# A hybrid decoder step on one core: sample y gathered in head pairs, fewer TensorE passes, and the sample states updated a token at a time on ScalarE and VectorE

## The chip, the cores and the metric

The kernel runs on one core of a Trainium2 chip. The time is device microseconds from launch to end, the median of several executions; lower is better. The core has TensorE (matrix products; PE in the profile, and PEld for its weight loads), VectorE (DVE), ScalarE (ACT), GpSimd (POOL) and SyncE (SP). In this kernel SP issues nearly all loads, POOL most stores, and each engine runs its instructions in the order in which they were emitted.

## The reference

One layer of a decoder step, for 256 prompt tokens and 8 sample sequences of 4 tokens each, 288 tokens in all. D_MODEL is 2048.

```python
h = rmsnorm(x)
u|v, z, xBC, dt, ga, gb = split(h @ w_in)
ya = u * (W_s @ layernorm(v) + b)                 # branch A, spatial gating
xs, B, C = split(silu(causal_conv(xBC)))          # branch B, Mamba-2: 64 heads, 8 groups
dt = softplus(dt + dt_bias); da = dt * -exp(a_log)
y = chunked_scan(xs, dt, da, B, C, h0) + d_skip * xs
yb = group_rmsnorm(y * silu(z))
x = x + (sigmoid(ga) * (ya @ w_out_a) + sigmoid(gb) * (yb @ w_out_b)) @ w_o
x = x + (silu(h2 @ w_gate) * (h2 @ w_up)) @ w_down   # h2 = rmsnorm(x)
y_out = rmsnorm(x)
```

The scan also gives the states after the last token. For a sample sequence that is, for each head, `state = state * exp(sum of da) + sum over its 4 tokens of (decayed dt*x) outer B`, with a state of 64 x 128 per head: 16 MB read and 16 MB written over the 8 sequences and 64 heads. This is the update that the change moves off TensorE.

## The kernel before, in words

All activations lie with channels in partitions and the 288 tokens in the free dimension. Every large product streams a weight matrix once, in units of 256 output columns. SP loads raw fp32 weights, 4 k (512 KB) at a time, into four buffers. ScalarE rounds each such piece to `wh` (line 183) and VectorE takes the rest `wl = raw - wh` (line 152); TensorE then makes three products of 288 columns for each 128x128 weight tile: `wh` with the high and the low part of the activations, and `wl` with the high part (line 187). So a piece is 24 products named pm, in one of two PSUM tiles ("m"). Three buffers hold `wh` and `wl`, and the split of a piece is emitted two pieces ahead, so a cast waits until the products of the piece three before it are done. The activations have names with h and l at the end: hh and hl for the normalised input, ybh and ybl for yb, xgh and xgl for the input of the FFN, fh and fl for its hidden layer.

The order of all engines is fixed when the program is built, by the class Plan. `units` walks through the units in an order written out by hand: v, dt, b, u, c, ga, the projection of branch A, then x and z, the first half of B (eight units, groups 0 to 3 of yb, one group for each piece), more x and z, gb, the second half of B, w_o, and the FFN. Between the k of a unit it calls `side`, which lets the generators of all other work run on: g_ssd, g_head, g_gate and so on, with priorities; the state update, g_upd, has the last but for nothing, 3, and starts at the mark "late", behind the z units. A generator goes on when the planner's own clocks say that what it waits for is ready, with a margin MG, and when VectorE and ScalarE are not planned more than SL = 2300 ns behind TensorE. Where TensorE is to use something that isn't emitted yet, `need` lets every generator run without that limit until it is. `res` and `rel` count the buffers: 25 large tiles q, 7 tiles t, 4 PSUM tiles x and 2 of m.

g_ssd prepares a group of 8 heads: cb = C'B, masked into cbm, the transposes btok, xt, xts, and the products for the prompt's last states (fin). g_head makes y of two heads (one of four pairs): a masked decay matrix m of 128 x 768, then on TensorE the sample's part from the old states (yoff times a selection), the sample's own part (a 32 x 64 slice of xts times a 32 x 32 block of ms), and the prompt's part (xt times m, 256 and 128 columns, for two halves of 64 rows). g_gate multiplies with silu(z), takes the group's mean square through a product with ones (rms) and a Newton iteration on VectorE and ScalarE, and writes ybh and ybl. g_upd forms, for each of 32 head pairs, the update of 8 states as two TensorE products of 512 columns (names up, from bk and sk), and VectorE adds them to the decayed states su, 8 instructions of 128x128; POOL stores 512 KB. At the end, fin_steps runs the prompt's last states while the final norm is taken, and SP stores y.

Of the kernel before, what the change touches and what calls it, by code (L numbers as in the profile page):

```python
# [6 lines left out]
F32 = mybir.dt.float32  # L7
# [50 lines left out]
class Plan:  # L58
# [216 lines left out]
    def rms(self, parts, scale, eps, out):  # L275
# [27 lines left out]
    def units(self, units, x_parts, first_loads):  # L303
# [35 lines left out]
        def split_to(i):  # L339
            while nxt[1] <= min(i, len(pieces) - 1):  # L340
# [3 lines left out]
                hi = self.wp.tile([128, NK, 256], F32R, tag="wh", name="wh")[:, 0:k1 - k0, 0:m]  # L344
                lo = self.wp.tile([128, NK, 256], F32R, tag="wl", name="wl")[:, 0:k1 - k0, 0:m]
# [3 lines left out]
                wt[nxt[1]] = (hi, lo)  # L349
# [6 lines left out]
        for i, (u, k0, k1, r, o) in enumerate(pieces):  # L356
# [28 lines left out]
def trunk(ctx, tc, io):  # L385
# [238 lines left out]
    def g_dt(ps):  # L624
# [200 lines left out]
    def g_ssd(g):  # L825
# [66 lines left out]
        yield ms  # L892
        K.mul(ms, ms, cbm[:, 384:416].unsqueeze(1).to_broadcast([128, 2, S]))
# [9 lines left out]
        for hf in range(2):  # L903
# [4 lines left out]
            left = [2]  # L908
            for j2 in range(2):
                K.spawn(1, g_head(g, hf, j2, csb, cbm, ms, xts, xt, X, left))  # L910

    def g_head(g, hf, j2, csb, cbm, ms, xts, xt, X, left):
        j = 2 * hf + j2
        m = yield from K.q([2, 384], f"m{g}{j}")
        yield csb
        for c in range(2):
            K.add(m[:, :, 256 * c:256 * c + 128], csb[:, 2 * j2:2 * j2 + 2, 128 * c:128 * c + 128], neg)
        yield m
        for i in range(2):
            h = 8 * g + 2 * j + i  # L920
            K.act(m[:, i, 0:128], m[:, i, 0:128], AF.Exp, bias=ncs[:, 0, h:h + 1])
            K.act(m[:, i, 128:256], csb[:, 2 * j2 + i, 128:256], AF.Exp, bias=dec[:, h:h + 1])
            K.act(m[:, i, 256:384], m[:, i, 256:384], AF.Exp, bias=ncs[:, 1, h:h + 1])
            yield None
        left[0] -= 1
        if not left[0]:
            K.drop()
# [524 lines left out]
```

## Time and profile before

| what | value |
| --- | --- |
| median of 3 runs | 2328.21 us (2327.59 to 2328.46) |
| profiled execution, its time | 2328.14 us |
| its span, first to last instruction | 2326.4 us |
| TensorE busy | 2317.5 us |
| VectorE busy | 1423.4 us |
| ScalarE busy | 996.9 us |
| GpSimd busy | 89.6 us |
| mean DMA rate | 196 GB/s |

The busy times come from one profiled execution. TensorE's is the time with at least one product under way; products overlap, so one of 288 columns shows as some 300 ns while the next one starts 133 ns later. The difference between time and span lies before the first and behind the last instruction.

### The profile page before, as it was taken

The page shows a single profiled execution, that of the slowest core. Times are in us where ns is not written, and L with a number is a line of the kernel's source. Part 1 is how long each engine was busy: PE and PEld are TensorE (multiplying, and loading weights), DVE is VectorE, ACT ScalarE, POOL GpSimd, SP SyncE. Part 2 cuts the span into 40 slices and gives each one's busy share as a digit, 9 for nine tenths or more (in the row PEclk, how much of TensorE's full clock was granted, in tenths as well). Part 3 has the DMA queues.
Part 4 walks back from the last instruction along what each step waited for, and adds up shares of the span by engine and source line. Part 5 has one row for each costly group of instructions (what it writes and reads, how often), then busy time and mean ns, then how long its engine had stood idle before and what let it go on. Part 6 is the DMA issues. An engine that isn't in the chain of part 4 may idle for free.

```text
span 2326.4 us, 42350 instructions
## 1 busy us (share of the span) xinstructions
PE 2317.5 (100%) x17523; PEld 2280.3 (98%) x17523; DVE 1423.4 (61%) x2174; ACT 996.9 (43%) x1413; POOL 89.6 (4%) x187
## 2 busy tenths in 40 slices
PE   9999999999999999999999999999999999999998
PEld 8999989999999999999999999999999999999998
DVE  7687553446878775477765777766554444544544
ACT  6443433335655554455433334433333333333332
POOL 0000000001100010010000000000000000000000
PEclk9999999999999999999999999999999999999999
DMA  8464685566665565564577877776555555555654
GB/s 284 139 207 147 204 296 169 179 187 186 194 226 170 155 196 182 179 191 137 172 236 250 277 269 256 234 240 228 181 167 159 167 170 167 166 164 165 231 168 135
DMA packets 150530, 455.26 MB, mean 196 GB/s; under 512 B 18736, under 2 KB 40496, under 8 KB 150336
## 3 DMA queue, kind: packets, MB, share of 16 engines
q1 hardware_dynamic: 139952, 423.35, 58.0%
q0 software_dynamic: 9376, 27.62, 3.2%
q8 instruction: 137, 2.24, 0.4%
q10 hardware_dynamic: 1008, 1.58, 0.2%
q14 instruction: 57, 0.47, 0.1%
HBM read 420.94 MB, written 31.54 MB: 194 GB/s over the span
## 4 chain that ended last, share of the span: by engine, by line
PE 99%; DMA 0%; ACT 0%; DVE 0%; SPq 0%; issue 0%; ACTq 0%
PE pm L187 93%; PE y L187 2%; PE yoff L187 1%; PE up L187 1%; PE fin L187 1%; PE mix L187 0%; PE xt L193 0%; PE cb L187 0%; DMA x<-x 0%; PE rms L187 0%; PE va L193 0%; PE btok L193 0%; ACT wh L183 0%; PE cst L187 0%; SPq L197 0%; PE vb L193 0%
## 5 line engine op out<-in xcount | busy, mean ns | idle before, releaser
L152 DVE TENSOR_TENSOR wl<-raw,wh 128x1024 fp32r<-128x1024 f32 (+2 forms) x704 | 837.9, 1190 | 860.8 <-ACT wh L183 851.5
L183 ACT CAST wh<-raw 128x1024 fp32r<-128x1024 f32 (+2 forms) x704 | 718.6, 1021 | 1111.3 <-PE pm L187 812.5
L187 PE MATMUL pm<-hh,wh 128*128 128x288 f32 x2128 | 635.5, 299 | 0.0
L187 PE MATMUL pm<-hh,wl 128*128 128x288 f32 x2128 | 628.1, 295 | 0.0
L187 PE MATMUL pm<-hl,wh 128*128 128x288 f32 x2128 | 627.7, 295 | 0.0
L187 PE MATMUL pm<-xgh,wl 128*128 128x288 f32 x1408 | 415.7, 295 | 0.0
L187 PE MATMUL pm<-xgl,wh 128*128 128x288 f32 x1408 | 415.6, 295 | 0.0
L187 PE MATMUL pm<-xgh,wh 128*128 128x288 f32 x1408 | 414.7, 295 | 0.0
L187 PEld LDWEIGHTS pm<-hh,wh 128*128 128x128 f32 x2128 | 399.8, 188 | 10.0 <-issue 8.4
L187 PEld LDWEIGHTS pm<-hl,wh 128*128 128x128 f32 x2128 | 399.6, 188 | 0.7
L187 PEld LDWEIGHTS pm<-hh,wl 128*128 128x128 f32 x2128 | 399.6, 188 | 0.2 <-DVE wl L152 0.2
L187 PEld LDWEIGHTS pm<-xgl,wh 128*128 128x128 f32 x1408 | 264.5, 188 | 0.6
L187 PEld LDWEIGHTS pm<-xgh,wh 128*128 128x128 f32 x1408 | 264.3, 188 | 0.6
L187 PEld LDWEIGHTS pm<-xgh,wl 128*128 128x128 f32 x1408 | 264.4, 188 | 0.0
L187 PE MATMUL pm<-fl,wh 128*128 128x288 f32 x704 | 207.8, 295 | 0.0
L187 PE MATMUL pm<-fh,wl 128*128 128x288 f32 x704 | 207.8, 295 | 0.0
L187 PE MATMUL pm<-fh,wh 128*128 128x288 f32 x704 | 207.2, 294 | 0.0
L187 PE MATMUL pm<-ybh,wh 128*128 128x288 f32 x512 | 152.1, 297 | 0.0
L187 PE MATMUL pm<-ybh,wl 128*128 128x288 f32 x512 | 151.1, 295 | 0.0
L187 PE MATMUL pm<-ybl,wh 128*128 128x288 f32 x512 | 151.0, 295 | 0.0
L187 PEld LDWEIGHTS pm<-fl,wh 128*128 128x128 f32 x704 | 132.3, 188 | 0.0
L187 PEld LDWEIGHTS pm<-fh,wl 128*128 128x128 f32 x704 | 132.2, 188 | 0.0
(249 smaller groups left out, 2802.2 us busy)
## 6 DMA issues: line engine op xcount, KB each, us to landing
raw<-w_in SPq DMA_DIRECT2D x284, 512.0 KB, 3.9
raw<-w_gu SPq DMA_DIRECT2D x176, 512.0 KB, 3.8
raw<-w_d SPq DMA_DIRECT2D x75, 512.0 KB, 3.6
raw<-w_b SPq DMA_DIRECT2D x64, 512.0 KB, 4.6
st<-st_n SPq DMA_DIRECT2D x32, 512.0 KB, 7.7
raw<-w_a SPq DMA_DIRECT2D x32, 512.0 KB, 3.7
su<-st_p SPq DMA_DIRECT2D x32, 512.0 KB, 5.6
new_ssm_s<-su POOLq DMA_DIRECT2D x32, 512.0 KB, 4.3
```

The costliest lines, as they stand in the source:

```text
L152: self.nc.vector.tensor_tensor(out, a, b, op=op)
L183: self.nc.scalar.copy(out, a)
L187: self.nc.tensor.matmul(out, lhsT, rhs, start=start, stop=stop)
```

## The change

Five things change.

- The sample's y is made for two head pairs at once (g_heads). The 32 x 32 blocks become full-height products: cbz holds the blocks of cb in their own rows and zeros elsewhere, mz is ms times cbz, and yoff, xts and m are all multiplied in column halves of 64 with all 128 rows. It takes two PSUM tiles x and two tiles q at a time.
- The dt unit loads 64 columns of weights in place of 128 and packs their two parts side by side, so one product with the high and one with the low part of h gives both; ScalarE and VectorE add the halves.
- A mean square of one part is rounded and split (rmp) and multiplied with a rounded matrix of ones: two products at the rounded rate in place of one in fp32.
- The state update leaves TensorE. The states lie in 64 tiles, one for a group and a sequence, 128 x 4 x 128. For each, SP loads the state, the four rows of B broadcast over all partitions (bx) and 16 columns of the weighted x, which TensorE now transposes once a group (xwt). ScalarE scales the four parts by the decay, VectorE adds the four tokens, 16 instructions `su <- bx * x + su`, and POOL stores 256 KB. The tiles come from the pool t; one tile is loaded ahead.
- The planner gets a clock for the DMA queues, and a higher cost for a VectorE instruction with a scalar read from memory.

```diff
-        self.clk = dict(pe=0.0, dve=0.0, act=0.0, pool=0.0)
+        self.clk = dict(pe=0.0, dve=0.0, act=0.0, pool=0.0, dma=0.0)
...
     def stt(self, out, a, s, b, op0, op1):
         self.nc.vector.scalar_tensor_tensor(out=out, in0=a, scalar=s, in1=b, op0=op0, op1=op1)
-        self._at("dve", (free(out) + 66) / 0.96 + 61 * (not isinstance(s, float)), [out], [a, b])
+        self._at("dve", (free(out) + 66) / 0.96 + 140 * (not isinstance(s, float)), [out], [a, b])
...
         (eng or self.nc.sync).dma_start(out=out, in_=a)
-        self.rdy[out.tensor.name] = self.clk["pe"] + 4000
+        self._moved(out)
+        self.rdy[out.tensor.name] = self.clk["dma"] + 4000
     def store(self, out, a, eng=None):
         (eng or self.nc.gpsimd).dma_start(out=out, in_=a)
+        self._moved(a)
+    def _moved(self, a):
+        self.clk["dma"] = max(self.clk["dma"], self.clk["pe"]) + a.shape[0] * free(a) * 4 / 370
...
-        ps = self.ps("rms")
-        for i, part in enumerate(parts):
-            self.mm(ps[:, 0:T], self.one, part, i == 0, i == len(parts) - 1)
+        if len(parts) == 1:
+            w = self.tmp([128, 2, T], "rmp", F32R)
+            self.hilo(w[:, 0], w[:, 1], parts[0])
+            yield w
+            ps = self.ps("rms")
+            for i in range(2):
+                self.mm(ps[:, 0:T], self.oner, w[:, i], i == 0, i == 1, f32=False)
+        else:
+            ps = self.ps("rms")
+            for i, part in enumerate(parts):
+                self.mm(ps[:, 0:T], self.one, part, i == 0, i == len(parts) - 1)
...
-                hi = self.wp.tile([128, NK, 256], F32R, tag="wh", name="wh")[:, 0:k1 - k0, 0:m]
-                lo = self.wp.tile([128, NK, 256], F32R, tag="wl", name="wl")[:, 0:k1 - k0, 0:m]
+                wh = self.wp.tile([128, NK, 256], F32R, tag="wh", name="wh")[:, 0:k1 - k0]
+                hi = wh[:, :, 0:m]
+                if m == 64:
+                    lo = wh[:, :, m:2 * m]
+                else:
+                    lo = self.wp.tile([128, NK, 256], F32R, tag="wl", name="wl")[:, 0:k1 - k0, 0:m]
...
                 xh, xl = self.acts[key]
+                if m == 64:
+                    self.mm(ps[:, 0, 0:T], lo[:, k - k0], xh, k == 0, False, f32=False)
+                    self.mm(ps[:, 0, 0:T], lo[:, k - k0], xl, False, k == nk - 1, f32=False)
...
-        K.act(x, ps[0:64, 0, 0:T], AF.Identity, bias=vec[0:64, V_DT:V_DT + 1])
+        K.act(x, ps[64:128, 0, 0:T], AF.Identity, bias=vec[64:128, V_DT:V_DT + 1])
+        yield x
+        K.add(x, x, ps[0:64, 0, 0:T])
...
-        cbm = K.tmp([128, 416 + 2 * S], "cbm")
-        ms = cbm[:, 416:416 + 2 * S].rearrange("p (i t) -> p i t", i=2)
-        K.mul(cbm[:, 0:416], p1[:, 0:416], masks)
+        cbm = K.tmp([128, 512 + 2 * S], "cbm")
+        cbz = cbm[:, 384:512].rearrange("p (j t) -> p j t", j=4)
+        ms = cbm[:, 512:512 + 2 * S].rearrange("p (i t) -> p i t", i=2)
+        K.mul(cbm[:, 0:384], p1[:, 0:384], masks)
+        K.mul(cbz, p1[:, 384:416].unsqueeze(1).to_broadcast([128, 4, S]), own)
...
-        xw = K.tmp([128, 128], "xw")
+        xws = K.tmp([128, 2, 128], "xw")
+        xw, xwt = xws[:, 0], xws[:, 1]
         K.mul(pair(xw), pair(xts), wide(wds[:, H2]))
-        K.store(io["scr_xs"][g], xw)
+        yield xw
+        p1 = K.ps("xwt")
+        K.tr(p1[:, 0:128], xw)
+        yield p1
+        K.copy(xwt.rearrange("p (b j l) -> p j b l", b=NB, j=4), p1[:, 0:128].rearrange("p (j b l) -> p j b l", j=4, b=NB))
+        K.store(io["scr_xs"][g], xwt)
...
-            left = [2]
-            for j2 in range(2):
-                K.spawn(1, g_head(g, hf, j2, csb, cbm, ms, xts, xt, X, left))
-    def g_head(g, hf, j2, csb, cbm, ms, xts, xt, X, left):
...
+            K.spawn(1, g_heads(g, hf, csb, cbm, cbz, ms, xts, xt, X))
+    def g_heads(g, hf, csb, cbm, cbz, ms, xts, xt, X):
+        ms_, mz = [], []
+        for j2 in range(2):
+            t = yield from K.q([768 + 2 * S], f"m{g}{2 * hf + j2}")
+            ms_.append(t[:, 0:768].rearrange("p (i t) -> p i t", i=2))
+            mz.append(t[:, 768:768 + 2 * S].rearrange("p (i t) -> p i t", i=2))
+            if not j2:
+                yield csb
+            for c in range(2):
+                K.add(ms_[j2][:, :, 256 * c:256 * c + 128], csb[:, 2 * j2:2 * j2 + 2, 128 * c:128 * c + 128], neg)
+        for j2, m in enumerate(ms_):
+            yield m
+            for i in range(2):
+                h = 8 * g + 2 * (2 * hf + j2) + i
+                K.act(m[:, i, 0:128], m[:, i, 0:128], AF.Exp, bias=ncs[:, 0, h:h + 1])
+                K.act(m[:, i, 128:256], csb[:, 2 * j2 + i, 128:256], AF.Exp, bias=dec[:, h:h + 1])
+                K.act(m[:, i, 256:384], m[:, i, 256:384], AF.Exp, bias=ncs[:, 1, h:h + 1])
+                yield None
         K.drop()
+        for j2, m in enumerate(ms_):
+            yield m
+            K.mul(m, m, cbm[:, 0:384].unsqueeze(1).to_broadcast([128, 2, 384]))
+            K.mul(mz[j2], ms, cbz[:, 2 * hf + j2].unsqueeze(1).to_broadcast([128, 2, S]))
+        yield ms_ + [yoff]
+        yield from K.res("x", 2)
+        pys = [K.ps("y") for _ in range(2)]
+        halves = [(i, slice(64 * i, 64 * i + 64)) for i in range(2)]
+        for j2, py in enumerate(pys):
+            j = 2 * hf + j2
+            for i, o in halves:
+                K.mm(py[o, P:T], yoff[:, g % NY, 128 * j + 64 * i:128 * j + 64 * i + 64], sel, True, False)
+            for i, o in halves:
+                K.mm(py[o, P:T], xts[:, o], mz[j2][:, i], False, True)
+        for j2, py in enumerate(pys):
+            j = 2 * hf + j2
+            for c in range(2):
+                for i, o in halves:
+                    hc = slice(128 * j + 64 * i, 128 * j + 64 * i + 64)
+                    K.mm(py[o, 128 * c:P], xt[:, c, hc], ms_[j2][:, i, 256 * c:256 + 128 * c], c == 0, c == 1)
+        K.drop(2)
+        heads_done[g] = heads_done.get(g, 0) + 2
         if heads_done[g] == 4:
             K.drop()
             K.rel("t")
             if g % 4 == 3:
                 K.drop()
+        for j2, py in enumerate(pys):
+            j = 2 * hf + j2
+            yield py
+            K.stt(X[:, j], X[:, j], vec[:, V_DS + 4 * g + j:V_DS + 4 * g + j + 1], py[:, 0:T], ALU.mult, ALU.add)
+            K.rel("x")
+            evac_done[g] = evac_done.get(g, 0) + 1
+            if evac_done[g] == 4:
+                K.have.add(f"ssd{g}")
...
-    def g_upd(g):
...
+    def upd_load(n):
+        g, b = divmod(n, NB)
+        yield f"fin{g}"
         yield from K.res("t", 2)
+        st, w = K.tmp([128, 4, 128], "su"), K.tmp([128, 528], "bx")
+        K.load(st, io["st_p"][n])
+        K.load(w[:, 0:512].rearrange("p (l n) -> p l n", l=L), io["scr_bs"][g, L * b:L * b + L].partition_broadcast(128))
+        K.load(w[:, 512:528], io["scr_xs"][g, :, 16 * b:16 * b + 16])
+        return st, w
+    def g_upd():
+        yield "late"
+        nxt = yield from upd_load(0)
+        for n in range(64):
+            g, b = divmod(n, NB)
+            st, w = nxt
+            if n < 63:
+                nxt = yield from upd_load(n + 1)
+            yield [st, w]
+            for j in range(4):
+                K.act(st[:, j], st[:, j], AF.Copy, scale=etot[:, 4 * g + j, b:b + 1])
             yield st
+            for l in range(L):
+                for j in range(4):
+                    K.stt(st[:, j], w[:, 128 * l:128 * l + 128], w[:, 512 + 4 * j + l:513 + 4 * j + l], st[:, j],
+                          ALU.mult, ALU.add)
+                yield None
             yield st
+            K.store(io["new_ssm_s"][n], st)
+            K.rel("t", 2)
+        K.have.add("upd")
...
-        K.spawn(3, g_upd(g))
+    K.spawn(3, g_upd())
...
-    dev["w_dt"] = ca(wt[:, :, 14336:14464].transpose(1, 0, 2))
+    dev["w_dt"] = ca(wt[:, :, 14336:14400].transpose(1, 0, 2))
...
-    dev["st_p"] = ca(f["state_ssm"][0].reshape(8, 32, 128, 128).transpose(1, 2, 0, 3))
+    dev["st_p"] = ca(f["state_ssm"][0].reshape(8, 8, 4, 128, 128).transpose(1, 0, 3, 2, 4).reshape(64, 128, 4, 128))
```

The order of TensorE inside the first unit of B (B0), before, where the products of group 2 end and those of group 3 begin (the number behind ybh and ybl is that of the tile):

```order
L187 MATMUL pm<-ybh_8494,wh 128x288
L187 MATMUL pm<-ybl_8495,wh 128x288
L187 MATMUL pm<-ybh_8494,wl 128x288
L187 MATMUL pm<-ybh_8835,wh 128x288
L187 MATMUL pm<-ybl_8836,wh 128x288
L187 MATMUL pm<-ybh_8835,wl 128x288
```

And after the change, at the same place of B0:

```order
L187 MATMUL pm<-ybh_8921,wl 128x288
L193 MATMUL btok<-cst,bf 128x128 x2
L193 MATMUL btok<-cst,bf 32x128
L193 MATMUL xt<-cst,xs_8720 128x128 x8
L193 MATMUL xts<-cst,sm 128x128
L187 MATMUL rms<-rmp,oner 128x288 x2
L193 MATMUL xwt<-cst,xw 128x128
L187 MATMUL pm<-ybh_9460,wh 128x288
L187 MATMUL pm<-ybl_9461,wh 128x288
L187 MATMUL pm<-ybh_9460,wl 128x288
```

In the new order the transposes of g_ssd of a later group, the sum rms of group 3 itself and the transpose xwt stand directly ahead of its products, since all that g_gate does for group 3 is emitted there.

VectorE, before, at the place where ybl of group 3 (ybl_8836) is written, ahead of the first B unit; wl<-raw,wh is the low part of a weight piece:

```order
L170 SCALAR_TENSOR_TENSOR xs_7302<-xs_7302,vec,rbg 128x288 x4
L152 TENSOR_TENSOR wl<-raw,wh 128x1024
L170 SCALAR_TENSOR_TENSOR acc<-cb,cwh,acc 128x312 x2
L152 TENSOR_TENSOR ybl_8836<-xs_7302,ybh_8835 128x576
L170 SCALAR_TENSOR_TENSOR acc<-cb,cwh,acc 128x312
L152 TENSOR_TENSOR wl<-raw,wh 128x1024
L170 SCALAR_TENSOR_TENSOR acc<-cb,cwh,acc 128x312 x3
L152 TENSOR_TENSOR wl<-raw,wh 128x1024
L152 TENSOR_TENSOR ybl_8836<-xs_7302,ybh_8835 128x576
L727 MEMSET cb 128x2x3
```

After, the rows at whose end ybl of group 3 (ybl_9461) is written, behind the start of unit B0; rbg and nt are the Newton iteration, m the decay matrices of the next group:

```order
L170 SCALAR_TENSOR_TENSOR rbg<-nt,rbg 128x288
L152 TENSOR_TENSOR m_9432<-csb_9340,cst 128x2x128 x2
L152 TENSOR_TENSOR m_9435<-csb_9340,cst 128x2x128 x2
L152 TENSOR_TENSOR nt<-nt 128x288
L170 SCALAR_TENSOR_TENSOR nt<-nt 128x288
L170 SCALAR_TENSOR_TENSOR rbg<-nt,rbg 128x288
L170 SCALAR_TENSOR_TENSOR xs_7203<-xs_7203,vec,rbg 128x288 x4
L152 TENSOR_TENSOR m_9432<-m_9432,cbm 128x768
L152 TENSOR_TENSOR m_9432<-cbm 128x64
L152 TENSOR_TENSOR ybl_9461<-xs_7203,ybh_9460 128x576 x2
L152 TENSOR_TENSOR m_9435<-m_9435,cbm 128x768
L152 TENSOR_TENSOR m_9435<-cbm 128x64
```

Before, the four multiplications with rbg and the two ybl rows stood between weight splits of units ahead of B0. Now no weight split stands among these rows, which follow each other from the Newton iteration to ybl.

VectorE at the first units of the FFN, before; ff<-pm,rb reads a finished unit out of PSUM:

```order
L152 TENSOR_TENSOR nt<-nt 128x288
L170 SCALAR_TENSOR_TENSOR nt<-nt 128x288
L170 SCALAR_TENSOR_TENSOR rb<-nt,rb 128x288
L170 SCALAR_TENSOR_TENSOR su_16211<-su_16211,etot,up_16272 128x128 x4
L170 SCALAR_TENSOR_TENSOR su_16211<-su_16211,etot,up_16273 128x128 x4
L152 TENSOR_TENSOR wl<-raw,wh 128x1024
L152 TENSOR_TENSOR ff<-pm,rb 128x288 x2
L152 TENSOR_TENSOR wl<-raw,wh 128x1024 x2
L152 TENSOR_TENSOR ff<-ff 128x288
L152 TENSOR_TENSOR ff<-pm,rb 128x288 x2
```

After:

```order
L152 TENSOR_TENSOR nt<-nt 128x288
L170 SCALAR_TENSOR_TENSOR nt<-nt 128x288
L170 SCALAR_TENSOR_TENSOR rb<-nt,rb 128x288
L152 TENSOR_TENSOR wl<-raw,wh 128x1024
L170 SCALAR_TENSOR_TENSOR su<-bx,su 128x128 x16
L152 TENSOR_TENSOR ff<-pm,rb 128x288 x4
L152 TENSOR_TENSOR wl<-raw,wh 128x1024 x3
L152 TENSOR_TENSOR ff<-ff 128x288 x2
```

The 16 rows of a whole update tile now stand between a weight split and the rows that read the units out.

VectorE at the end of the program, before; x<-x,r is the last multiplication of the final norm:

```order
L166 TENSOR_SCALAR x_15914<-x_15914,vec 128x288
L152 TENSOR_TENSOR x_15014<-x_15014,r 128x288 x2
L152 TENSOR_TENSOR x_15014<-x_15014,r 128x576
L152 TENSOR_TENSOR x_15309<-x_15309,r 128x576 x2
L152 TENSOR_TENSOR x_15618<-x_15618,r 128x576 x2
L152 TENSOR_TENSOR x_15914<-x_15914,r 128x576 x2
```

After:

```order
L166 TENSOR_SCALAR x_16017<-x_16017,vec 128x288
L152 TENSOR_TENSOR x_15134<-x_15134,r 128x288 x2
L152 TENSOR_TENSOR x_15134<-x_15134,r 128x576
L152 TENSOR_TENSOR x_15433<-x_15433,r 128x576 x2
L152 TENSOR_TENSOR x_15725<-x_15725,r 128x576 x2
L152 TENSOR_TENSOR x_16017<-x_16017,r 128x576 x2
L170 SCALAR_TENSOR_TENSOR su<-bx,su 128x128 x48
```

The update of the last three tiles, 48 rows, stands behind the final norm.

## Rows read from the trace of the kernel before

**Rows 1.** The page: span, busy time of each engine, granted clock in 40 slices.
```profile
span 2326.4 us, 42350 instructions
...
PE 2317.5 (100%) x17523; PEld 2280.3 (98%) x17523; DVE 1423.4 (61%) x2174; ACT 996.9 (43%) x1413; POOL 89.6 (4%) x187
...
PEclk9999999999999999999999999999999999999999
```

**Rows 2.** The page: chain that ended last, share of the span by line.
```profile
PE pm L187 93%; PE y L187 2%; PE yoff L187 1%; PE up L187 1%; PE fin L187 1%; PE mix L187 0%; PE xt L193 0%; PE cb L187 0%; DMA x<-x 0%; PE rms L187 0%; PE va L193 0%; PE btok L193 0%; ACT wh L183 0%; PE cst L187 0%; SPq L197 0%; PE vb L193 0%
```

**Rows 3.** Chain in order of time, from 2270 us: start, us, what.
```profile
2269.89 37.52 PE pm L187 x282
...
2313.14 7.36 PE fin L187 x64
```

**Rows 4.** Timeline from 2302 us, VectorE, SP, ScalarE: start, us, engine, line.
```profile
2313.18 5.47 DVE L152 TENSOR_TENSOR x<-x,r 128x288 f32<-128x288 f32 x9 [1.58 <-PE r L187]
...
2313.66 7.21 SPq L201 DMA_DIRECT2D y<-x  x9
...
2321.13 0.34 ACTq L201 DMA_DIRECT2D new_ssm_p<-fin  x1
```

**Rows 5.** Chain in order of time, from 1160 us, the update.
```profile
1165.45 0.46 PE up L187 x2
```

**Rows 6.** Chain in order of time, from 560 us, y and rms.
```profile
640.65 2.56 PE y L187 x28
...
668.29 0.48 PE rms L187 x2
```

**Rows 7.** Timeline from 620 us, one head's y on TensorE.
```profile
620.21 0.30 PE L187 MATMUL y<-cst,yoff 128*128 128x32 f32 x2
...
620.45 0.30 PE L187 MATMUL y<-cbm,xts 32*64 32x32 f32 x4
...
620.68 0.88 PE L187 MATMUL y<-m,xt 128*64 128x256 f32 x8
```

**Rows 8.** Groups of VectorE by shape: count | busy us, mean ns | idle before.
```profile
L152 DVE TENSOR_TENSOR wl<-raw,wh 128x1024 fp32r<-128x1024 f32 x663 | 811.2, 1224 | 820.0 <-ACT wh L183 811.0 <-DMA b<-scr_bs 2.6 <-PE pm L187 2.0
...
L170 DVE SCALAR_TENSOR_TENSOR su<-su,etot,up 128x128 f32<-128x128 f32 x256 | 70.1, 342 | 0.9 <-PE up L187 0.9
...
L152 DVE TENSOR_TENSOR ff<-pm,rb 128x288 f32<-128x288 f32 x88 | 35.9, 449 | 0.0
...
L152 DVE TENSOR_TENSOR ybl<-xs,ybh 128x576 fp32r<-128x576 f32 x16 | 11.9, 752 | 0.0
...
L170 DVE SCALAR_TENSOR_TENSOR xs<-xs,vec,rbg 128x288 f32<-128x288 f32 x32 | 14.7, 513 | 0.0
...
L152 DVE TENSOR_TENSOR xt<-xt,dtk 128x512 f32<-128x512 f32 x16 | 10.9, 686 | 2.8 <-PE xt L193 2.8
```

**Rows 9.** Busy time by stretch: us, PE, PEld, DVE, ACT, POOL, PEclk, DMA share, GB/s.
```profile
1900.00:2000.00 100.00, 100.00 (x755) 100.00 (x755) 50.49 (x64) 38.30 (x48) 0.00 (x0) 1.00 0.56 167
...
2300.00:2326.40 26.40, 20.48 (x170) 20.07 (x168) 10.79 (x30) 5.16 (x9) 0.00 (x0) 0.94 0.42 155
```

**Rows 10.** Groups of ScalarE by shape, columns as in rows 8.
```profile
L183 ACT CAST wh<-raw 128x1024 fp32r<-128x1024 f32 x663 | 694.6, 1048 | 1061.4 <-PE pm L187 769.5 <-issue 260.1 <-DMA raw<-w_in 6.8
...
L178 ACT ACTIVATE m<-m,ncs 128x128 f32<-128x128 f32 x128 | 46.9, 390 | 1.0 <-DVE m L152 0.9
```

**Rows 11.** Timeline of the first 6.6 us, TensorE.
```profile
1.52 3.78 PE L411 MATMUL warm<-warm 128*128 128x512 f32 x4 [1.52 <-DVE warm L408]
...
6.41 0.29 PE L187 MATMUL pm<-x1h,wl 128*128 128x288 f32 x1
```

**Rows 12.** DMA issues: count, KB each, median us to landing.
```profile
raw<-w_gu SPq DMA_DIRECT2D x176, 512.0 KB, 3.8
...
new_ssm_s<-su POOLq DMA_DIRECT2D x32, 512.0 KB, 4.3
...
new_ssm_p<-fin ACTq DMA_DIRECT2D x6, 256.0 KB, 3.6
```

More of the change, by code (lines that the diff above doesn't have):

```diff
@@ L16 @@
 EPS = 1e-6
-C_ID, C_TRI, C_ONE, C_M32, C_SUF, C_MB, C_MBS, C_PAR, C_JM, C_BM, C_SEL, C_NEG, C_MP = (
-    0, 128, 256, 512, 544, 672, 704, 736, 864, 896, 904, 936, 1064)
-C_W = 1192
+C_ID, C_TRI, C_ONE, C_SUF, C_MB, C_MBS, C_PAR, C_JM, C_SEL, C_NEG, C_MP, C_JB = (
+    0, 128, 256, 512, 640, 672, 704, 832, 864, 896, 1024, 1152)
+C_W = 1280
 V_G1, V_G2, V_GF, V_NG, V_DS, V_CW, V_CB, V_DT, V_AL = 0, 16, 32, 48, 80, 112, 304, 352, 353
@@ L166, in ts @@
         self.nc.vector.tensor_scalar(out=out, in0=a, scalar1=s1, op0=op0, **kw)
-        self._at("dve", (free(out) / 2 + 66) / 0.96 + 61 * (not isinstance(s1, float)), [out], [a])
+        self._at("dve", (free(out) / 2 + 66) / 0.96 + 140 * (not isinstance(s1, float)), [out], [a])
     def stt(self, out, a, s, b, op0, op1):
         self.nc.vector.scalar_tensor_tensor(out=out, in0=a, scalar=s, in1=b, op0=op0, op1=op1)
-        self._at("dve", (free(out) + 66) / 0.96 + 61 * (not isinstance(s, float)), [out], [a, b])
+        self._at("dve", (free(out) + 66) / 0.96 + 140 * (not isinstance(s, float)), [out], [a, b])
     def vcopy(self, out, a):
@@ L413, in trunk @@
     tri = cst[:, C_TRI:C_TRI + 128]
+    K.oner = K.const([128, 128], "oner", F32R)
     sacc = K.const([128, T], "sacc")
@@ L477, in g_sgu_tables @@
         yield "unit2"
+        K.copy(K.oner, K.one)
         K.act(cwh, vec[:, V_CW:V_CW + 240], AF.Copy, scale=0.5)
@@ L787, in trunk @@
     yoff = K.const([128, NY, 512], "yoff")
-    masks = cst[:, C_TRI:C_TRI + 416]
+    masks = cst[:, C_TRI:C_TRI + 384]
+    own = cst[:, C_JB:C_JB + 128].rearrange("p (j t) -> p j t", j=4)
     sel = cst[:, C_SEL:C_SEL + 32]
@@ L891, in g_ssd @@
         K.act(ms, ms, AF.Exp)
-        yield ms
-        K.mul(ms, ms, cbm[:, 384:416].unsqueeze(1).to_broadcast([128, 2, S]))
         if g >= ND:
@@ L907, in g_ssd @@
                 yield csb
-            left = [2]
-            for j2 in range(2):
-                K.spawn(1, g_head(g, hf, j2, csb, cbm, ms, xts, xt, X, left))
-    def g_head(g, hf, j2, csb, cbm, ms, xts, xt, X, left):
[L913 to L927, printed above, removed]
-        yield m
-        K.mul(m, m, cbm[:, 0:384].unsqueeze(1).to_broadcast([128, 2, 384]))
-        yield [m, ms, yoff]
-        yield from K.res("x")
-        py = K.ps("y")
-        K.mm(py[:, P:T], yoff[:, g % NY, 128 * j:128 * j + 128], sel, True, False)
-        for i in range(2):
-            o = slice(64 * i, 64 * i + 64)
-            K.mm(py[o, P:T], xts[32 * j:32 * j + 32, o], ms[32 * j:32 * j + 32, i], False, True)
-        for i in range(2):
-            o = slice(64 * i, 64 * i + 64)
-            hc = slice(64 * (2 * j + i), 64 * (2 * j + i) + 64)
-            K.mm(py[o, 0:P], xt[:, 0, hc], m[:, i, 0:256], True, False)
-            K.mm(py[o, 128:P], xt[:, 1, hc], m[:, i, 256:384], False, True)
-        K.drop()
-        heads_done[g] = heads_done.get(g, 0) + 1
@@ L948, in g_head @@
                 K.drop()
-        yield py
-        K.stt(X[:, j], X[:, j], vec[:, V_DS + 4 * g + j:V_DS + 4 * g + j + 1], py[:, 0:T], ALU.mult, ALU.add)
-        K.rel("x")
-        evac_done[g] = evac_done.get(g, 0) + 1
-        if evac_done[g] == 4:
-            K.have.add(f"ssd{g}")
+        for j2, py in enumerate(pys):
[6 more added lines that the diff above has]
+                K.have.add(f"ssd{g}")
     heads_done, evac_done = {}, {}
@@ L1030, in trunk @@
-    K.have.add("upd-1")
+        st, w = K.tmp([128, 4, 128], "su"), K.tmp([128, 528], "bx")
[14 more added lines that the diff above has]
+                K.act(st[:, j], st[:, j], AF.Copy, scale=etot[:, 4 * g + j, b:b + 1])
+            yield st
+            for l in range(L):
[3 more added lines that the diff above has]
+                yield None
+            yield st
+            K.store(io["new_ssm_s"][n], st)
+            K.rel("t", 2)
+        K.have.add("upd")
@@ L1329, in trunk @@
     K.need("end")
-    for i in range(8):
-        K.need(f"upd{i}")
+    K.need("upd")
 def _constants():
@@ L1352, in _constants @@
     c[at, C_SEL + s] = 1
-    c[:, C_M32:C_M32 + 32] = np.tile(blk & (s[:, None] <= s[None, :]), (4, 1))
+    for j in range(4):
+        c[32 * j:32 * j + 32, C_JB + 32 * j:C_JB + 32 * j + 32] = blk & (s[:, None] <= s[None, :])
     h = i[:64]
@@ L1380, in _layout @@
     vec[:, V_CB:V_CB + 48] = chan(f["conv_b"][0])
-    vec[:64, V_DT] = f["dt_bias"][0]
+    vec[64:, V_DT] = f["dt_bias"][0]
     vec[:64, V_AL] = f["a_log"][0]
```

48 lines of the change are left out of this document (4 added, 44 removed).

## The prediction

> **What bounds the kernel now.** I read the page first. TensorE is busy for 2317.5 us of a 2326.4 us span, and its granted clock stands at 9 tenths or more in all 40 slices; VectorE is busy for 1423.4 us, 61% [rows 1]. The chain that ended last is TensorE all the way, 93% of it the dense weight products pm [rows 2]. Read in order of time, that chain gives the pace: 282 pm products in a row take 37.52 us, 133 ns each [rows 3], and no piece of it before the tail belongs to another engine. So two things can change the time: passes that TensorE is spared or given, and waits that TensorE gets, of which it has none now. The end is a second stage: TensorE stops near 2320.5 [rows 3], the y stores leave from 2313.66 for 7.21 us, and VectorE's last work ends at 2313.18 + 5.47 = 2318.65 [rows 4].
>
> The profiled execution took 2328.14 us, 1.74 us more than its span, and the median shown is 2328.21. I sum against the span and add 1.74. A measurement of this kernel tells about 0.2%, 4.7 us, from no change.
>
> **What TensorE saves.** The state update's products go: 32 tiles, two products each, 0.46 us a pair [rows 5]: −14.9 us. The dt unit makes two passes for three at each of 16 k: 16 × 133 ns = −2.1. Nine sums of squares have one part and go from one fp32 product (two records, 0.48 us [rows 6]) to two rounded ones at the pm pace (0.27): −1.9. Eight transposes of xw come in at the pace of a 128-column pass, 7.36 us / 64 = 0.115 [rows 3]: +0.9.
>
> The sample's y in pairs is not so plain. A pair of heads costs 2.56 us now [rows 6]. One head's timeline [rows 7] shows its parts start at 620.21, 620.45 and 620.68, the last in 0.88 us. A 128-column fp32 pass is 0.115 us, 0.9 ns a column, so the 32-column products of the first two parts hold little work; most of their 0.47 us is the change from 128x128 to 32x64 to 128x64 tiles. The new pair changes shape twice where the old one does so six times, worth up to 0.7 us; but its small products become 16 records with 128-row weights, whose loads at some 0.05 each could eat all of it. Both ends are open, so I take the middle, 0.34 a pair, 16 pairs: −5.5 (0 to −11). The 8 wide passes of a head stand in 0.88 us [rows 7], where four of 256 and four of 128 columns would take 1.38 one after the other: the halves of the array already work side by side, so writing them in alternation gives nothing there. The Trainium skill (TensorE: Matmul & The Clock Gate, Part 3: Packing small matmuls — row/col tiling) says that products on distinct column groups run concurrently, and gives 2.38x for three of them; were they serial now, that rule would make the alternation worth some 0.5 us a head, 16 us in all, and I price that as a rival below. The row decides against it.
>
> Savings together: 14.9 + 2.1 + 1.9 + 5.5 − 0.9 = **23.5 us** (18 to 29).
>
> **What VectorE gets.** The update becomes 64 tiles of 16 instructions. The 256 old ones are busy for 70.1 us, 274 ns each, with a mean duration of 342 [rows 8]; the new ones have the same shape and both tensors in SBUF: 1024 × 0.274 = 281 us in, 70 out, some 19 of preparation out: +190 over 1150 us. From 1900 to 2000 VectorE is at 50% [rows 9]; 16 to 25 points more is no bound as a mean. ScalarE gets 256 scalings of 128 elements near 46.9 / 128 = 0.37 [rows 10]: +94, from 38%. SP's loads and POOL's stores move the same 16 MB, plus 16 MB of broadcasts, under a DMA share of 0.56. As a mean all this is hidden. What isn't hidden is order: each engine runs its instructions as emitted, so I walked VectorE's order wherever TensorE waits for something emitted shortly ahead. Three places stand out.
>
> **Wait A, unit B0.** Each B unit takes one group's yb in each of its four pieces. Before, group 3's ybl was written long ahead. Now it comes 35 rows of VectorE's order after group 2's, and between the third piece and the fourth TensorE has only the head's bursts. Time 0 is the end of the second piece, when a weight buffer comes free; durations by size [rows 8]: 1.22 for 1024 elements, 0.95 for 768 (between its neighbours), 0.75 for 576, 0.69 for 512, 0.51 or 0.45 for some 300, and 0.25 for 128 and less (the su rows, rounded). Cast 1.05 [rows 10], wl 1.22, three acc 1.53, m 0.95 and 0.25, first ybl 0.75: 5.8, where the third piece can begin. Then m and the second ybl 1.95 (7.7), eight xs rows 2.4, two 1.0, one 0.75, cbm 0.8: 12.7. The third piece with its y pair and short products ends near 12.3, so its buffer gives the next cast and wl at 14.6. Then xs 0.75, xt 1.38, z 1.2, xd 1.38, xts, rmp and xw 0.95: 20.3. Then the Newton rows of group 3, seven of 0.45, with four m additions 1.8, four xs 2.05, a small pair 0.5, m 1.2 and the first ybl 0.75: **29.6**. TensorE's own work in that stretch is 48 − 24 products 3.2, a y pair 2.4, cb 0.8 and some 18 short passes 2.0: 8.4. The loss is 21; I take **20**. The lower bound is 14: only the part after the third piece, 17.3, with every row a fifth shorter (as 274 is to 342). The upper is 24, with handovers between engines added.
>
> **Wait B, first FFN unit.** The last xgl stands behind a wl that waits for its buffer, and behind four update rows. From the buffer: 1.05 + 1.22 + 4 × 0.258 + 0.75 = 4.05 (0.258 if they follow each other a little closer than the 274 of the table); TensorE has 14 products, 1.87, of its own: **2.4** with handovers (1 to 3.5).
>
> **Wait C, third FFN unit.** It needs a PSUM tile that ff<-pm,rb must free. Those stand behind a wl pinned to the end of the unit before and 16 update rows: 1.05 + 1.22 + 16 × 0.258 + 2 × 0.45 = 7.3; **7.2** (5.5 to 8.5). Before, ff follows a wl with no update row between.
>
> **The clock.** In the last 26.4 us the mean granted clock is 0.94 [rows 9], which is some 3 us at the half level (1.2 of 2.4 GHz): it fell near 2323, and TensorE had last worked at 2320.5. At the start, four passes of 512 columns take 3.78 us, 0.9 each and twice the later pace (4 × 0.115 is 0.46); the products reach 0.29 us at 6.41, some 4.5 us after the first [rows 3, 11]. The waits of 5.8, 9 and 7 us are longer than the idle end of the trace, so I expect two returns at 1.2 GHz, some 4 us long as at the start, 2 us lost in each: **+4** (0 to 6.3). The Trainium skill (the same page, Part 1: The HAM clock gate) says that the throttled state is the default and that activity releases it; that speaks for this term, and no row of before has such a wait inside the run.
>
> **The tail.** The last three tiles' 48 update rows stand after the y multiplications that end at 2318.65, and the last tile's load after SP's nine y stores. 48 × 0.258 to 0.274 = 12.4 to 13.2: 2331.1 to 2331.8. Then a store of 256 KB, which lands in 3.6 us from ScalarE's queue, where one of 512 KB from POOL takes 4.3 [rows 12], with some 0.5 to issue. Today's last store leaves at 2321.13 [rows 4] and should land near 2324.8, so some 1.5 us follow a landing: 2336.7 to 2338.1 against 2326.4: **+11** (8 to 15).
>
> **Sum.** 2326.4 − 23.5 + 20 + 2.4 + 7.2 + 4 + 11 = 2347.5 of span, 2349.2 with what lies around it.
>
> **Rivals.** *Shorter waits and no fall of the clock*: A at 14, B at 1, C at 5.5, tail 9, clock 0: 2326.4 − 23.5 + 29.5 + 1.7 = 2334. For it: VectorE's table means contain pauses. 15%. *SP held by the update's loads*: in SP's order the load of a tile waits for the store of the tile two before, and weight loads queue behind it. Against it: a weight load lands in 3.8 us [rows 12] and four raw buffers hold 12.8 us. It decides once a hold exceeds some 8 us; a quarter of a microsecond for each of 64 tiles gives 2365. 13%. *Other side, A hidden*: VectorE and ScalarE reach unit B0 with room, as the emitter's limit SL of 2.3 us intends, so A and its clock fall vanish, and B and C shrink to nothing: 2326.4 − 23.5 + 11 + 1.7 = 2316. It decides when A + B + C + clock stay under 12.5. Against it: the casts in that stretch are tied to TensorE's own progress by three weight buffers, so VectorE can't be ahead. 7%. *The halves were serial* (the rule above): the forecast less 16 − 5.5, 2339. 3%. That *the pairs save nothing* gives 2355, inside the range.
>
> **How the numbers follow.** The forecast, 2349.2, has 62%; its own range, from the terms' bounds not all at one end, is 2340 to 2358. For eight in ten I reach down to the short waits, 2333, and up towards the held queue, 2362; outside stay the other side and half of the held queue. Faster by over 0.2%: the other side and a little of chance, 0.08. Within 0.2% (2323.6 to 2332.9): what lies below the short waits, 0.07. Slower: 0.85.
>
> **What would show it.** Right: pm waits of over 10 us on DVE ybl in unit B0, one of 2 us on xgl and one of 7 us on ff in the first FFN units; clock slices below 9 just there; up gone from the chain; a last chain of 48 su rows, POOL store, end. Wrong: TensorE without a wait at B0; waits on weight casts spread over the FFN, releaser a raw load (the held queue); y pairs of 2.5 us or of 1.5.

## The result, and the profile after

The changed kernel takes 2347.24 us (median of 4 runs, 2346.05 to 2348.10), beside 2327.9 for the kernel before: a ratio of 1.0081, interval 1.0069 to 1.0093. It is slower by 0.8%, where 2349.2 us was predicted. In the profiled runs the last pm product starts 6.8 us later than before, and the span ends 18.7 us later: so 6.8 us on TensorE, and 11.9 behind it.

The page of the changed kernel, the same lines as [rows 1]:

```profile
span 2345.1 us, 43710 instructions
...
PE 2297.0 (98%) x17515; PEld 2264.6 (97%) x17515; DVE 1611.9 (69%) x2952; ACT 1072.0 (46%) x1673; POOL 106.2 (5%) x219
...
PEclk9999999999999989999999999999999999999998
```

TensorE has 20 us less to do and takes longer. VectorE is at 69%, which alone bounds nothing. Apart from the last slice, in which TensorE stops, one slice of 40, near 850 us, has a lower clock. What TensorE waits for, in all: total us, times, longest. The first row is from before, the largest of waits that came to 2.8 us in all; the others are from after.

```profile
PE warm L411 <- DVE warm L408: 1.5, 1, 1.5
...
PE pm L187 <- ACT ybh L183: 8.3, 2, 6.8
PE pm L187 <- DVE ff L152: 7.3, 1, 7.3
PE pm L187 <- DVE ybl L152: 4.8, 2, 3.7
PE rms L187 <- ACT rmp L183: 4.4, 1, 4.4
PE pm L187 <- DVE xgl L152: 2.0, 1, 2.0
...
PE rms L187 <- DVE rmp L152: 0.9, 1, 0.9
```

The rows on ybh, ybl and rmp are wait A, 18.4 us; xgl is B, ff is C. Together 27.7 us in a handful of waits: the rest of the FFN has none. Wait A seen from VectorE, in its timeline (start, us, and in brackets the idle time ahead of it):

```profile
835.62 1.22 DVE L152 TENSOR_TENSOR wl<-raw,wh 128x1024 fp32r<-128x1024 f32 x1
...
839.25 0.75 DVE L152 TENSOR_TENSOR ybl<-xs,ybh 128x576 fp32r<-128x576 f32 x1
...
849.57 1.23 DVE L152 TENSOR_TENSOR wl<-raw,wh 128x1024 fp32r<-128x1024 f32 x1 [1.07 <-ACT wh L183]
...
861.35 1.80 DVE L170 SCALAR_TENSOR_TENSOR xs<-xs,vec,rbg 128x288 f32<-128x288 f32 x4
...
864.07 1.42 DVE L152 TENSOR_TENSOR ybl<-xs,ybh 128x576 fp32r<-128x576 f32 x2
```

With time 0 at the end of the second piece, 834.2, group 2's first ybl ends at 5.8, the next wl at 16.6 and group 3's first ybl near 30.6; the prediction had 5.8, 14.6 and 29.6. VectorE is idle for less than 5 of these 30.6 us. It isn't overloaded by the update, whose first row on VectorE starts at 1171.7 us, 300 us later: it has one long chain to do after TensorE already needs its end. Wait C in the same view, VectorE and then TensorE:

```profile
1490.05 1.22 DVE L152 TENSOR_TENSOR wl<-raw,wh 128x1024 fp32r<-128x1024 f32 x1 [0.61 <-ACT wh L183]
1491.20 4.28 DVE L170 SCALAR_TENSOR_TENSOR su<-bx,su 128x128 f32<-128x128 f32 x16
1495.40 1.54 DVE L152 TENSOR_TENSOR ff<-pm,rb 128x288 f32<-128x288 f32 x4
...
1496.36 0.58 PE L187 MATMUL pm<-xgh,wh 128*128 128x288 f32 x1 [7.33 <-DVE ff L152]
```

The clock by stretch (the column behind the engines is the mean granted clock, as in [rows 9]):

```profile
842.00:845.00 3.00, 3.00 (x28) 2.07 (x26) 1.80 (x7) 0.00 (x0) 0.00 (x0) 0.52 0.00 0
...
863.00:866.00 3.00, 1.73 (x5) 1.41 (x6) 3.00 (x6) 0.84 (x2) 0.00 (x0) 0.50 0.01 3
866.00:869.00 3.00, 3.00 (x14) 2.90 (x13) 1.17 (x4) 0.00 (x0) 0.00 (x0) 0.54 0.02 5
869.00:871.00 2.00, 2.00 (x35) 1.48 (x33) 0.55 (x2) 0.00 (x0) 0.00 (x0) 1.00 0.00 0
...
1473.00:1476.00 3.00, 3.00 (x14) 3.00 (x14) 0.99 (x3) 0.96 (x2) 0.00 (x0) 0.50 0.93 285
...
1498.00:1500.00 2.00, 2.00 (x10) 2.00 (x10) 0.00 (x0) 0.00 (x0) 0.00 (x0) 0.50 0.00 0
```

Behind A's waits, behind B and behind C TensorE works on at the half level: from 840.05, where a wait of 3.7 us ends, to 845; from 863.22 to about 868.7, with a wait of 1.05 inside; from 1472.76, where B ends, to about 1476.4; from 1496.36 to about 1500.1. At that level the pm products start 240 ns apart and not 133, so 45% of the time is lost: 2.2, 2.0, 1.6 and 1.7 us, 7.5 in all.

The end, VectorE and then POOL, the lines that answer to [rows 4]:

```profile
2319.97 5.47 DVE L152 TENSOR_TENSOR x<-x,r 128x288 f32<-128x288 f32 x9 [1.58 <-PE r L187]
2325.36 8.48 DVE L170 SCALAR_TENSOR_TENSOR su<-bx,su 128x128 f32<-128x128 f32 x32
2335.22 4.29 DVE L170 SCALAR_TENSOR_TENSOR su<-bx,su 128x128 f32<-128x128 f32 x16 [1.39 <-DMA bx<-scr_xs]
...
2339.81 0.54 POOL L202 DMA_DIRECT2D new_ssm_s<-su  x1 [5.14 <-DVE su L170]
```

48 update rows at 0.265 us each run after all else that VectorE does, and the last tile's bx, loaded late, costs 1.4 us more.

### The profile page after: what moved, and what is told of

Same layout as the page of the kernel before. It is cut to its first block, busy times and chain, and to the rows that moved or that the text cites. A ratio compares the mean times of both kernels' runs of the same rounds, so it can differ in the third digit from the quotient of the medians.

```text
span 2345.1 us, 43710 instructions
## 1 busy us (share of the span) xinstructions
PE 2297.0 (98%) x17515; PEld 2264.6 (97%) x17515; DVE 1611.9 (69%) x2952; ACT 1072.0 (46%) x1673; POOL 106.2 (5%) x219
## 5 line engine op out<-in xcount | busy, mean ns | idle before, releaser
L170 DVE SCALAR_TENSOR_TENSOR su<-bx,su 128x128 f32<-128x128 f32 x1024 | 286.5, 343 | 1.4 <-DMA bx<-scr_xs 1.4
```

## The experiments

The theory is that the change's work pays, and that the waits and the tail come from the order in which the emitter, with its new clocks, puts that work. The main rival is load: 190 us more on VectorE, and SP's queue held for stores. Some experiments undo a part of the change, others steer the emitter. All compute the whole step.

**1. Both of the emitter's clocks as before, all else of the change kept.**

```diff
-        self._at("dve", (free(out) + 66) / 0.96 + 140 * (not isinstance(s, float)), [out], [a, b])
+        self._at("dve", (free(out) + 66) / 0.96 + 61 * (not isinstance(s, float)), [out], [a, b])
...
-        self.rdy[out.tensor.name] = self.clk["dma"] + 4000
+        self.rdy[out.tensor.name] = self.clk["pe"] + 4000
```

The cost of 140 goes back to 61 in `ts`, the helper beside it, too.

> The whole change, but the emitter's clocks as before (pointer cost 61, a load ready 4 us after TensorE's clock). My theory: the waits and the late tail come from the order that the new clocks plan, not from the new work. With the old clocks the emitted order has group 3's ybl ahead of B0, a unit's worth of room before the first FFN unit, and no update row behind the last product. So the waits of 27.7 us, the clock's 5.7 and the tail's 11.9 all go: 2347.2 - 45.3 = 2302 us, at most 2306. Rival, load: VectorE has 190 us more to do and SP holds its queue for stores 128 times, so TensorE waits wherever it works; then this order does little, 2335 to 2350.

Measured: 2310.36 us, ratio 0.9926 (0.9911 to 0.9941). The same work in another order is 0.7% faster than the kernel before, and the load rival falls. But 8 us of the forecast were missing. The waits that are left, behind those of the start:

```profile
PE pm L187 <- DVE ff L152: 8.7, 1, 8.7
```

A, B and the tail are gone; C isn't, which I had counted as gone with the rest. It is made elsewhere, as run 4 shows.

**2. The heads one pair at a time as before (g_head), new clocks and update kept.**

> The change with the sample y one head pair at a time as before, all else new, new clocks too. The emitted order has group 3's ybl 47 products ahead of its use, but the first FFN units and the 48 update rows behind the last product stand as in the changed kernel. My theory: wait A and its clock go (18.4 + 4.2), B, C and tail stay (9.3 + 1.5 + 11.9), and the pairs' 9.8 us come back: 2347.2 - 22.6 + 9.8 = 2334 us. Rival, the pairs themselves make A by taking two PSUM and two q tiles: same time here, but then the first run still waits at B0. Rival, load: 2347 + 9.8 = 2357.

Measured: 2333.77 us, ratio 1.0021 (1.0011 to 1.0030), as my theory had it. Only B and C are left:

```profile
PE pm L187 <- DVE ff L152: 7.3, 1, 7.3
PE pm L187 <- DVE xgl L152: 2.0, 1, 2.0
```

Run 1 kept the pairs and run 2 the clocks, and neither has A: with the update moved, it takes both, since either alone gives another order. (Run 8 has A with the old clocks, in another order again.)

**3. The state update as before (g_upd with its TensorE products), new clocks and pairs kept.**

> The change with the state update as before on TensorE, all else new, new clocks too. The order has group 3's yb still right ahead of its use (one product), group 2's no longer, no update rows ahead of ff, none behind the last product. My theory: A stays for its second part (some 12 to 18 us with its clock), B, C and tail go (9.3 + 1.5 + 11.9), the 14.9 of the up products come back: 2347.2 - 22.7 + 14.9 - (0 to 7) = 2333 to 2340 us. Rival, load on VectorE is what costs: with 190 us less on VectorE all waits go, A too: 2328 - 12 = 2316.

Measured: 2319.54 us, ratio 0.9965 (0.9950 to 0.9979): a miss on the number, by 13 us. Wait A was shorter than the 12 to 18 us that I read from the order, 6.1 + 0.8, but it was there, with 190 us less on VectorE:

```profile
PE pm L187 <- ACT ybh L183: 6.1, 1, 6.1
```

So A doesn't need the update's load. With A at this length and 2.6 us of half clock behind it, the sum of the expectation gives some 2326 us; the half clock behind B, which it left out, takes 1.6 more off, and the other 5 us of the miss are open. How long A gets can't be told from the one product that stands between the write and the use.

**4. The changed kernel, but no update emitted while TensorE's next product waits for something not yet emitted.**

```diff
-            self.side(slack=1e9)
+            self.side(slack=1e9, top=9 if key in ("end", "upd") else 2)
```

Here `side` skips generators whose priority is above top.

> The changed kernel, except that the planner emits no update while TensorE's next product waits for something not yet emitted (other work alone runs on there). So the 16 update rows ahead of ff in the third FFN unit move behind it; A and B stand as before, and 64 update rows instead of 48 stand behind the last product. My theory: C and its clock go (7.3 + 1.5) and the tail gets one more tile (4.2, with its load up to 6): 2343 to 2345 us. Rival, C is VectorE's load in the FFN and not these 16 rows: the wait appears again a unit later, 2347 to 2353.

Measured: 2341.2 us, ratio 1.0056 (1.0041 to 1.0071), 6 us less than the changed kernel and 2 below the forecast. The wait on ff falls to what is left here, and no other takes its place:

```profile
PE pm L187 <- DVE ff L152: 1.3, 1, 1.3
```

So `need` puts the 16 rows there: it lets every generator run without the limit SL until ff is emitted, the lowest priority too. The span now ends 35.6 us behind the last pm product, 4.4 more than with 48 rows. What is below the forecast is B, 1.0 us here in place of 2.0, and the clock, which falls neither behind B nor behind C: ff −6.0, B −1.0, the clock −1.6 and −1.7, the tail +4.4, together −5.9 us, against −6.0 measured.

**5 to 8. Both together (old clocks, update held), and that with one part undone each.**

> The whole change with the old clocks, and the update held back while TensorE's next product waits for something not yet emitted. The run with old clocks alone was at 2310.4 us with a single wait left, 8.7 us on ff in the third FFN unit, and about 1.5 us at the half clock behind it. My theory: the 16 update rows ahead of ff are all of it, as in the run with the new clocks, where the wait fell to 1.3: 2310.4 - 7.4 - 1.5 = 2301.5 us (2299 to 2304). Rival, load in the FFN: the wait moves to the next units, 2308 to 2312.

> As the run beside it (old clocks, update held), but the sample y one head pair at a time as before. No wait of TensorE differs in the emitted order, so the difference is the price of the pairs alone. From the traces a pair of pairs takes 2.01 us against 2.55 to 2.65: 16 x 0.54 to 0.64 = 8.6 to 10.2 us more than the run beside it. Rival, my predicted term: 5.5 us more. Rival, the halves ran at once already and nothing is won: 0.

> As the first run here (old clocks, update held), but the nine sums of one part in one fp32 product as before. From the traces an fp32 product of 288 columns puts 0.271 us between the dense products and the two rounded ones put 0.266, so I expect the same time within 0.5 us. My prediction had 0.48 against 0.27 each: by that 1.9 us more than the first run.

> As the first run here (old clocks, update held), but the state update as before on TensorE. 32 pairs of up products come back, 0.467 us each, 14.9 us; eight transposes of 0.03 us go; the 1.3 us left of the wait on ff go. In this order group 3's yb again stands one product ahead of its use, so a wait of some 7 us at B0 comes with it. So 2301.5 + 14.9 - 1.5 + 7 = 2322 us; without that wait 2315. Rival, load: an update on VectorE costs as much as it saves on TensorE, 2302 plus the wait.

Measured, on one chip: 2307.39 (ratio 0.9905, 0.9890 to 0.9920); with the old heads 2316.66 (0.9945, 0.9933 to 0.9958); with the old sums 2307.38 (0.9908, 0.9895 to 0.9922); with the old update 2331.28 (1.0011, 1.0002 to 1.0020).

Run 5 missed by 6 us: a wait of 4.6 us stayed ahead of the third FFN unit. The 16 update rows were 4.1 of run 1's 8.7 us; the rest is the chain of the FFN norm's Newton rows, which ff needs, and which stands late in the order of run 1 already. ScalarE and then VectorE in run 5:

```profile
1462.88 1.28 ACT L178 ACTIVATE su<-su,etot 128x128 f32<-128x128 f32 x4
1464.06 0.43 ACT L178 ACTIVATE nt<-rb 128x288 f32<-128x288 f32 x1
1465.11 1.04 ACT L183 CAST wh<-raw 128x1024 fp32r<-128x1024 f32 x1 [0.62 <-ACT nt L178]
...
1466.19 1.23 DVE L152 TENSOR_TENSOR wl<-raw,wh 128x1024 fp32r<-128x1024 f32 x1 [1.96 <-ACT wh L183]
1467.33 0.45 DVE L152 TENSOR_TENSOR nt<-nt 128x288 f32<-128x288 f32 x1
```

Four scalings of the update stand ahead of ScalarE's row of the chain, but that row is done at 1464.49, and VectorE's next one starts at 1467.33: the order puts it behind a second weight split, whose cast keeps to TensorE's pace (casts start at 1458.74, 1461.92 and 1465.11).

Run 6 against run 5 gives the price of the pairs alone, 9.3 us, as the traces have it and not my 5.5. Run 7 shows no difference, but my expectation for it was worked out wrongly: I had looked at where the product behind rms starts, and not at the one after it. The old sum takes 0.48 us with the gap behind it, the new one 0.26, so nine sums save 2.0 us of TensorE in the traces, as predicted (1.9); in run 7 the wait on ff is also 1.1 us shorter, probably since the new sum puts a cast and a subtraction into that chain, and the executions of a run scatter over 3 to 4 us. That leaves the sums unsettled, between 0 and 2 us. Run 8 tells nothing of the update's price: in that order A came back with 12.5 us where I had 7, though the clocks are the old ones, with these among its waits:

```profile
PE y L187 <- DVE m L152: 5.2, 2, 4.0
PE rms L187 <- ACT rmp L183: 5.0, 1, 5.0
```

So the new clocks aren't the only way to A. The runs without the pairs, 2 and 6, have none of it.

**9. Only the DMA clock as before, the pointer cost at 140.**

> The whole change, with only the DMA clock taken back (a load ready 4 us after TensorE's clock); the pointer cost stays at 140. It tells which of the two new clocks orders the waits. The emitted order still has group 3's yb one product ahead of its use, xgl one product ahead, 16 update rows ahead of ff, and 52 update rows behind the last product. My theory: the pointer cost, which makes the planner see VectorE as full, is what holds other work back; so A stays in its second part at least (7 to 18 us), B, C (9) and the tail (12 to 13): 2333 to 2345 us. Rival: the DMA clock is it, and the time falls to that of both old clocks, 2310.

Measured: 2345.01 us, ratio 1.0074 (1.0058 to 1.0091). A is there with 14 us of waits, and the wait on ff takes 8.7, so neither needs the DMA clock. Run 1 differs from this run in the pointer cost alone and takes 2310.36 us: with the DMA clock as before, that cost by itself brings some 35 us. The fourth combination, 61 with the new DMA clock, was not run, so whether that clock alone would bring such an order is open.

**10. The changed kernel, no update emitted from the last two units of w_o to the third FFN unit.** `self.quiet` is true for those units.

```diff
-            if g[0] > 0 and behind > (slack or self.SL):
+            if g[0] > 0 and behind > (slack or self.SL) or g[0] > 2 and self.quiet:
                 continue
```

> The changed kernel with its new clocks, but no update emitted from the last two units of w_o to the third FFN unit. A stands as before, nothing of the update is near B and C, and 96 update rows, not 48, stand behind the last product. My theory: TensorE gains B, C and their clock, 2.0 + 7.3 + 1.5 = 10.8, and the tail grows by three tiles of 4.2 to 4.6, 13.2: 2347.2 - 10.8 + 13.2 = 2349.6 us (2348 to 2352). Rival, the tail is bound by the last loads or stores and not by the 16 rows of each tile: it stays near 31 us behind TensorE's last product, 2336.

Measured: 2348.09 us, ratio 1.0087 (1.0072 to 1.0102). B and C are gone from the waits, and what TensorE gained VectorE gives back behind the final norm:

```profile
2313.68 8.48 DVE L171 SCALAR_TENSOR_TENSOR su<-bx,su 128x128 f32<-128x128 f32 x32
2324.13 16.89 DVE L171 SCALAR_TENSOR_TENSOR su<-bx,su 128x128 f32<-128x128 f32 x64 [1.97 <-DMA bx<-scr_bs]
```

The span ends 31.2, 35.6 and 44.4 us behind the last pm product with 48, 64 and 96 rows (the changed kernel and runs 4 and 10): 4.4 us a tile. The tail is VectorE's rows, not a store.

**11. Old clocks, old sums, and the same quiet stretch.**

> The change with the old clocks, the sum of squares as before, and no update emitted from the last two units of w_o to the third FFN unit. In the order ff then stands 29 products ahead of its use. The run with old clocks, update held and old sums was at 2307.4 us with one wait left, 3.5 us and some 1.8 behind it. My theory: that wait goes and nothing takes its place: 2302 us (2300 to 2304), 1.1% below the kernel before. Rival: the wait is the FFN norm's own chain and stays without the update, 2305 to 2308.

Measured: 2302.24 us, ratio 0.9890 (0.9875 to 0.9904): faster than both kernels, 45 us below the changed one. All of TensorE's waits:

```profile
PE warm L428 <- DVE warm L425: 1.5, 1, 1.5
PE va L194 <- ACT gv L179: 0.5, 1, 0.5
PE pm L188 <- ACT x1h L179: 0.4, 1, 0.4
PE rms L188 <- DVE sq L153: 0.3, 1, 0.3
PE yoff L188 <- DMA st<-st_n: 0.2, 1, 0.2
```

The same 1024 update rows run here, and VectorE is at 70%. The norm's chain is still there, but with no update emitted near it the order has one weight split between its two iterations, where run 5 had two.

## Why the prediction was right

By its own steps, term by term of the sum:

| term | predicted | measured |
| --- | --- | --- |
| what TensorE saves | −23.5 | −28.4 |
| wait A | +20 | +18.4 |
| wait B | +2.4 | +2.0 |
| wait C | +7.2 | +7.3 |
| clock | +4 | +7.5 |
| tail | +11 | +11.9 |

The first row is summed from the traces: 14.9, 2.1 and 1.9 as predicted, 10.4 for the pairs, less 0.9 for the transposes. The measured terms sum to 18.7, and the span grew by 18.7, but the terms aren't as exact as that. Run 11, which has no waits to speak of, has its last pm product 25.1 us earlier than before, where −28.4 without the 1.9 of the sums would give 26.5: there 1.4 are missing, so the first row is probably a little high, and the waits, which the view counts from the end of a record of 0.29 us though the next product could start after 0.13, are a little low. That the forecast came within 2 us of the measured time is in part luck: the savings were 4.9 us larger than predicted and the clock cost 3.5 us more, and the two nearly cancel.

- **The savings.** The mis-sized term is the pairs: 5.5 taken, the middle between two open ends, 10.4 in the traces (16 times two head pairs, at 2.11 us against 2.76, from the product ahead to the second behind, less two paces) and 9.3 in run 6. Two head pairs of the changed kernel, on TensorE, against the one in [rows 7]:

```profile
631.82 0.31 PE L187 MATMUL y<-cst,yoff 128*64 128x32 f32 x4
631.96 0.29 PE L187 MATMUL y<-m,xts 128*64 128x32 f32 x4
632.07 0.29 PE L187 MATMUL y<-cst,yoff 128*64 128x32 f32 x4
632.19 0.29 PE L187 MATMUL y<-m,xts 128*64 128x32 f32 x4
632.30 1.50 PE L187 MATMUL y<-m,xt 128*64 128x256 f32 x16
633.74 0.40 PE L187 MATMUL pm<-hh,wh 128*128 128x288 f32 x1
```

  The 16 small records take 0.48 us for two head pairs, where six took 0.47 for one: near the upper end, since a small record costs 0.03 and not the 0.05 that could have eaten the gain. The wide passes take 1.44 for two head pairs, where one took 0.81, so they win little. That writing the halves in alternation would be a large gain is refuted here: they worked side by side already. The sums and the transposes came out as predicted (0.22 less each; 0.11 each).
- **A, B, C** were right in place and size, and B and C in what releases them. The sign named for A, over 10 us on ybl, did not come: 4.8 of its 18.4 us are on ybl, 8.3 on ScalarE's ybh just ahead of it in the same chain, and 5.3 on rmp further ahead. That A comes from order was right; what makes the order the prediction left open. With the update moved, runs 1, 2 and 9 give it: the higher pointer cost together with the pairs.
- **The clock** is the other mis-sized term, at 7.5 us also above its bound of 6.3. It fell more often than I took it to, four times and not two: one stretch at the half level followed A's first wait, and the y pair of B0 fell into it, and one followed B's 2.0 us. (In the profiled execution of run 2 the same wait of 2.0 us has none behind it.) The rule of the Trainium skill (TensorE: Matmul & The Clock Gate, Part 1: The HAM clock gate), that activity releases a throttled default, agrees with the stretches above.
- **The tail** was 0.9 us longer, by the last tile's late load.
- **The rivals.** Against "A hidden" stood that the casts tie VectorE to TensorE, and that held: ScalarE had sat idle for 7.9 us, until pm gave a weight buffer back, before the cast for the wl at 849.57. SP did wait for the update's buffers, but TensorE waited for no weight, as predicted; one cast, of w_d, waited 4.0 us for its load (the changed kernel's SP, total, times, longest):

```profile
SPq L197 <- DVE su L170: 353.5, 128, 4.3
```

## What to carry to other kernels

Where a planner's table of costs decides the order of engines, a change to the table is a change to the kernel: take it back alone before the rest of the change is judged. Moving work off the bounding engine pays only where the new work can't get between that engine and what it waits for; look for places that emit without a limit (here, whatever fills a wait), and keep low-priority work out of them. Work that is spread over spare time must be done before the end, or each piece left over adds its full length there.

## What the runs showed of the hardware

- A tuned stream of products lost its full clock in each of four stretches of waiting, 5.3 us with one product inside, some 13 us with four, 2.0 us and 7.3 us, and each time worked on for 3.6 to 5.5 us at the half level, with its products 240 ns apart in place of 133. On top of 27.7 us of waits that is some 7.5.
- One instruction `su <- bx * x + su` of 128x128 with both tensors in SBUF takes 0.265 us in a row of 32, though its record says 0.343; with one tensor in PSUM the table of before gives 0.274 [rows 8].
- An fp32 product among rounded ones costs nearly as much behind it as in it. TensorE's timeline of run 7:

```profile
677.65 0.65 PE L187 MATMUL rms<-z,cst 128*128 128x288 f32 x2
677.92 0.51 PE L187 MATMUL pm<-hh,wh 128*128 128x288 f32 x1
678.28 0.30 PE L187 MATMUL pm<-hl,wh 128*128 128x288 f32 x1
678.41 0.29 PE L187 MATMUL pm<-hh,wl 128*128 128x288 f32 x1
```

  The next dense product starts 0.27 us after it, but the second only 0.36 us after the first, where 0.13 is the pace.
